# Longer rows and buffers for TensorE's float32r operands in a four-layer hybrid decoder trunk

## The chip, the core and the metric

The kernel runs on one core of a Trainium2 chip. The metric is the device time in microseconds (us) of one execution. TensorE (PE in the views) multiplies and transposes, and its weight loads are shown as an engine of their own (PEld). VectorE (DVE), ScalarE (ACT) and GpSimd (POOL) work elementwise, and SyncE's queue (SP) carries the weights from HBM.

## The reference, cut to what matters

A decoder of four layers works on 256 tokens of 1024 features in float32. Each layer adds a token mixer and an MLP to the running x:

```
for i in range(4):
    x = x + mixer[i % 3](rmsnorm(x) * norm1[i])     # retention, MoBA, differential, retention
    u = relu((rmsnorm(x) * norm2[i]) @ w_up[i])     # 1024 -> 4096
    x = x + (u * u) @ w_down[i]                     # 4096 -> 1024
```

Retention has four heads with keys of 256 and values of 512 features and a gate. The two attentions have sixteen heads of 64 features, a relative position bias and a norm of q and k per head. Each mixer has a projection in (1024 to 6144 or 3072) and one out.

## The kernel before, in words

**Precision.** The big products are made in float32r, TensorE's faster form of float32. To keep the accuracy, each operand is split into a high part (a copy rounded to float32r) and a low part (what is left). `passes` (L296) then issues three matmuls for each product: high by high, high weights by low moving, low weights by high moving. In every call of PE.matmul, lhsT is the stationary operand, which is loaded as weights (128 columns), and rhs is the moving operand that streams past it (256 or 512 columns).

**Weights.** `load_raw` brings one megabyte at a time into one of three buffers `raw`. `split_piece` (L153) lets ScalarE copy half of it into `whi`, `split_lo` (L167) lets VectorE subtract to get `wlo`. There are six buffers of each, 4096 bytes per partition, used in turn; `advance` keeps the split four pieces ahead of the matmuls.

**Activations.** The normed x is transposed and split into `xhi` and `xlo` (`norm_new` L262, `norm_quarter` L266), eight rows (k) of 256 tokens each, 1024 bytes per row. Retention and attention leave their output in `oh` and `ol` (four rows each). The MLP leaves the squared hidden units in `uu` (`act_u`, L375): rows 0 and 1 are high, 2 and 3 low.

**Which operand is which.** In `mm_a` (the up projection, `up`, and retention's q and k, `qk`), the weights are slices of `whi` and `wlo`, and a row of `xhi` or `xlo` moves, 256 columns. In `mm_b` (`vg` and `qkv`), slices of `xhi` and `xlo` are the weights, and `whi` or `wlo` moves, 512 columns. In `mm_o` (the projections out and down, `acc`), slices of `uu` or `oh` and `ol` are the weights, and `whi` or `wlo` moves, 512 columns. In retention's `av` (L444) the scores `s2` are the weights, and `vh` or `vl` moves, 512 columns; its output is called `o`.

**Order.** The order of all work is written out by hand (`manual_schedule`). The MLP does `up(s + 1)`, 48 matmuls, ahead of the 24 matmuls `acc` of slice s, so `uu` of one slice is made while the next slice's up projection runs. Small work (transposes `xt`, `oT`, `qkT`, attention scores `sc`, all in float32) is put between these runs by `later` and `tick`.

**Addresses.** The pools lie one behind the other in the order in which they are opened (const, op, xp, up, wp, mp, rp), and every tile takes a multiple of 32 bytes per partition. This puts the beginning of each of `oh`, `ol`, `xhi`, `xlo`, `uu`, `vh`, `vl`, `whi` and `wlo` at remainder 32 modulo 128, and the slices taken from them start at multiples of 512 bytes from there. Only `s2`, in the pool mp behind fifteen small tiles of 32 bytes, begins at remainder 0.

Of the kernel before, what the change touches and what calls it, by code (L numbers as in the profile page):

```python
# [10 lines left out]
F32R = mybir.dt.float32r  # L11
# [5 lines left out]
P = 128  # L17
S = 256
# [3 lines left out]
KC = D // P  # L22
# [9 lines left out]
def trunk(ctx, tc, x_in, rel_bias, norm1, norm2, w_up, w_down, ret_w_in, ret_w_out,  # L32
# [8 lines left out]
    op_ = ctx.enter_context(tc.tile_pool(name="op", bufs=1))  # L41
    xp = ctx.enter_context(tc.tile_pool(name="xp", bufs=1))
    up_ = ctx.enter_context(tc.tile_pool(name="up", bufs=1))
    wp = ctx.enter_context(tc.tile_pool(name="wp", bufs=1))
# [7 lines left out]
    NRAW, NPC = 3, 6  # L52
# [4 lines left out]
    def aux_bank(name):  # L57
        return pa.tile([P, 512], F32, tag="aux", name=name)
# [11 lines left out]
    def run_due():  # L70
        while True:
            due = [p for p in pending if p[0] <= clock[0]]
            if not due:
                return
            p = min(due, key=lambda p: p[:3])
            pending.remove(p)
            p[3](*p[4])

    def tick():
        clock[0] += 1  # L80
        run_due()


    specs = []

# [63 lines left out]
    def parts(i, n):  # L149
        m = n if i else n // 2  # L150
        return [slice(c, c + m) for c in range(0, n, m)]

    def split_piece():  # L153
        i = nxt[1]
        r = i // 2
        if r >= len(specs):
            return
        nxt[1] += 1
        _, a, b = specs[r]
        half = raws[r][:, (i % 2) * (a // 2):(i % 2 + 1) * (a // 2), :]  # L160
        hi = wp.tile([P, a // 2, b], F32R, tag="hi", name="whi", bufs=NPC)
        lo = wp.tile([P, a // 2, b], F32R, tag="lo", name="wlo", bufs=NPC)
        for part in parts(i, a // 2):
            ACT.activation(hi[:, part], half[:, part], AF.Copy)  # L164
        pieces[i] = (hi, lo, half)
# [13 lines left out]
    def advance(ah=4, al=4):  # L179
        while True:  # L180
            a, b = nxt[1], nxt[3]
            if nxt[1] <= nxt[2] + ah and nxt[1] // 2 < len(specs):
                split_piece()
            if nxt[3] <= nxt[2] + al:
                split_lo()
            if (a, b) == (nxt[1], nxt[3]):
                return
# [8 lines left out]
    rows = mp.tile([32, P], F32, tag="t2k", name="rows", bufs=4)  # L196
# [63 lines left out]
    st = {}  # L260

    def norm_new():  # L262
        st["hi"] = xp.tile([P, KC, S], F32R, tag="xhi", name="xhi")
        st["lo"] = xp.tile([P, KC, S], F32R, tag="xlo", name="xlo")

    def norm_quarter(l, which, c, t):  # L266
        tt = slice(t * P, (t + 1) * P)
# [33 lines left out]
    def mm_a(ps, half, first_of_phase=False):  # L301
        if not first_of_phase:
            advance()
        hi, lo = take()
        for m in range(2):
            for kk in range(4):
                k = half * 4 + kk
                passes(ps[:, m * S:(m + 1) * S], hi[:, kk, m * P:(m + 1) * P], lo[:, kk, m * P:(m + 1) * P],
                       st["hi"][:, k, :], st["lo"][:, k, :],
                       half == 0 and m == 0 and kk == 0, half == 1 and m == 1 and kk == 3)  # L310
                if first_of_phase and m == 0 and kk == 2:
                    tick()
        tick()
# [16 lines left out]
    def acc_new():  # L330
        st["acc"] = {q: mm_bank("acc") for q in QUARTERS}
# [9 lines left out]
    def out_piece(src, first):  # L341
        advance()
        pc = take()
        for q in QUARTERS:
            mm_o(q, pc, src, first, False)
        tick()

    def finish(srcs, r2, nxt_norm):
        advance(4, 4)
        pcs = [take() for _ in srcs]  # L350
        if nxt_norm is not None:
            norm_new()
        for q in QUARTERS:
            for i, (pc, src) in enumerate(zip(pcs, srcs)):
                mm_o(q, pc, src, False, i == len(srcs) - 1)
            c, t = q
            xs = X[:, t, c * 512:(c + 1) * 512]
            ps = st["acc"][q]
            if r2 is None:
                DVE.tensor_tensor(xs, ps, xs, op=OP.add)  # L360
            else:
                DVE.scalar_tensor_tensor(xs, ps, r2[:, t:t + 1], xs, op0=OP.mult, op1=OP.add)
            if nxt_norm is None:
                nc.sync.dma_start(out.rearrange("b s d -> (b s) d")[t * P:(t + 1) * P, c * 512:(c + 1) * 512], xs)
            else:
                later(2, norm_quarter, nxt_norm[0], nxt_norm[1], c, t)
            tick()
        if nxt_norm is not None:
            later(3, rms, nxt_norm[1])


    def mlp(l):
        U = {}

        def act_u(s, ps):  # L375
            u = mp.tile([P, 512], F32, tag="t2k", name="u", bufs=4)
            ACT.activation(u, ps, AF.Relu)  # L377
            DVE.scalar_tensor_tensor(u, ps, 0.0, u, op0=OP.max, op1=OP.mult)  # L378
            uu = up_.tile([P, 4, S], F32R, tag="p4k", name="uu", bufs=6)
            uh, ul = uu[:, 0:2, :], uu[:, 2:4, :]  # L380
            uf = u.rearrange("p (m s) -> p m s", m=2)
            ACT.activation(uh, uf, AF.Copy)
            DVE.tensor_tensor(ul, uf, uh.bitcast(F32), op=OP.subtract)
            U[s] = [(uh[:, m, :], ul[:, m, :]) for m in range(2)]

        def up(s):
            ps = aux_bank("up")
            mm_a(ps, 0, s == 0)
            mm_a(ps, 1)
            act_u(s, ps)  # L390

        up(0)
        acc = False
        for s in range(16):
            if s + 1 < 16:
                up(s + 1)
            if not acc:
                acc_new()
                acc = True
            if s < 14:  # L400
                for m in range(2):
                    out_piece(U[s][m], s == 0 and m == 0)
                del U[s]
            elif s == 14:
                out_piece(U[s][0], False)
            else:
                finish([U[14][1]] + U[15], st["r2"], (l + 1, 0) if l + 1 < DEPTH else None)


    def retention(l):  # L410
        OT = {}
        kd = mp.tile([P, 8, S], F32, tag="kd", name="kd")
# [61 lines left out]

        def to_feat(h, e, t):
            if h not in OT:
                OT[h] = (op_.tile([P, 4, S], F32R, tag="ot%d" % h, name="oh"),
                         op_.tile([P, 4, S], F32R, tag="ol%d" % h, name="ol"))
            ps = aux_bank("oT")
            for i in range(4):  # L480
                PE.transpose(ps[:, i * P:(i + 1) * P], e["go", t][:, i * P:(i + 1) * P], ident)
            v = ps.rearrange("p (i s) -> p i s", i=4)
            hi = OT[h][0][:, :, t * P:(t + 1) * P]
            lo = OT[h][1][:, :, t * P:(t + 1) * P]
            ACT.activation(hi, v, AF.Copy)
            DVE.tensor_tensor(lo, v, hi.bitcast(F32), op=OP.subtract)
# [31 lines left out]
        for c in range(13):  # L518
            h, i = divmod(c, 4)
            out_piece((OT[h][0][:, i, :], OT[h][1][:, i, :]), c == 0)  # L520
        finish([(OT[3][0][:, i, :], OT[3][1][:, i, :]) for i in (1, 2, 3)], None, (l, 1))
# [35 lines left out]
    def attention(l):  # L557
# [12 lines left out]
        def at(tk, fn, *a):  # L570
            later(max(t0 + 1 + tk - clock[0], 0), fn, *a)
        V = [up_.tile([P, D], F32, tag="p4k", name="vt", bufs=6) for _ in range(2)]
        OT = [(op_.tile([P, 4, S], F32R, tag="ot%d" % (2 + b), name="oh"),
               op_.tile([P, 4, S], F32R, tag="ol%d" % (2 + b), name="ol")) for b in range(2)]
        if diff:
            lambda_full()
        qs = qsc[:, 1:2] if diff else qsc[:, 0:1]
# [178 lines left out]


    norm_new()
    for t in range(2):
        norm_quarter(0, 0, 0, t)  # L760
    split_piece()
    split_lo()
    for t in range(2):
        later(1, norm_quarter, 0, 0, 1, t)
    later(1, split_piece)
    later(1, split_lo)
    later(3, rms, 0)
    later(10, head_weights)
    for l in range(DEPTH):
        if l % 3 == 0:  # L770
            retention(l)
        else:
            attention(l)
        mlp(l)
# [43 lines left out]
```

## Time and profile before

| | |
|---|---|
| median of 3 runs | 1371.81 us (1371.8 to 1372.04) |
| profiled execution, its own time | 1371.75 us |
| its span, first to last instruction | 1370.0 us |
| TensorE busy in the span | 1355.8 us, 99% |
| VectorE, ScalarE, GpSimd busy | 62%, 50%, 8% |
| mean granted TensorE clock | 0.999 of full speed |

The span is 1.75 us shorter than the execution's own time. A matmul's listed duration reaches from its start to a modelled end and overlaps the next one, so a run of matmuls is read by the distance between starts.

### The profile page before, as it was taken

The page shows a single profiled execution, that of the slowest core. Times are in us where ns is not written, and L with a number is a line of the kernel's source. Part 1 is how long each engine was busy: PE and PEld are TensorE (multiplying, and loading weights), DVE is VectorE, ACT ScalarE, POOL GpSimd, SP SyncE. Part 2 cuts the span into 40 slices and gives each one's busy share as a digit, 9 for nine tenths or more (in the row PEclk, how much of TensorE's full clock was granted, in tenths as well). Part 3 has the DMA queues.
Part 4 walks back from the last instruction along what each step waited for, and adds up shares of the span by engine and source line. Part 5 has one row for each costly group of instructions (what it writes and reads, how often), then busy time and mean ns, then how long its engine had stood idle before and what let it go on. Part 6 is the DMA issues. An engine that isn't in the chain of part 4 may idle for free.

```text
span 1370.0 us, 19714 instructions
## 1 busy us (share of the span) xinstructions
PE 1355.8 (99%) x7956; PEld 1190.5 (87%) x7956; DVE 846.8 (62%) x1246; ACT 689.6 (50%) x1063; POOL 109.1 (8%) x316
## 2 busy tenths in 40 slices
PE   7999999999999999999999999999999999999998
PEld 6888889999987779999987789999988888899997
DVE  6666647555568856555578675555667675555554
ACT  5454436444456645444466754444455444544442
POOL 3111100000032000000021100000031011000000
PEclk9999999999999999999999999999999999999999
DMA  8545464555565336555554346555564555465551
GB/s 279 178 159 180 163 206 159 188 189 190 195 208 167 124 123 219 185 185 184 185 173 136 123 154 215 185 185 184 169 207 144 180 182 188 151 216 186 185 185 62
DMA packets 140796, 242.26 MB, mean 177 GB/s; under 512 B 4256, under 2 KB 87920, under 8 KB 140704
## 3 DMA queue, kind: packets, MB, share of 16 engines
q1 hardware_dynamic: 137872, 236.99, 51.5%
q0 software_dynamic: 1072, 2.35, 0.6%
q10 hardware_dynamic: 1760, 1.66, 0.4%
q8 instruction: 62, 1.02, 0.3%
q14 instruction: 30, 0.25, 0.1%
HBM read 239.91 MB, written 1.07 MB: 176 GB/s over the span
## 4 chain that ended last, share of the span: by engine, by line
PE 98%; ACT 1%; DVE 0%; DMA 0%; issue 0%; ACTq 0%
PE acc L297 12%; PE acc L298 12%; PE acc L299 12%; PE up L299 9%; PE up L298 9%; PE up L297 9%; PE vg L297 4%; PE vg L299 4%; PE vg L298 4%; PE qkv L297 3%; PE qkv L299 3%; PE qkv L298 3%; PE qk L299 2%; PE qk L297 2%; PE qk L298 2%; PE sc L635 1%
## 5 line engine op out<-in xcount | busy, mean ns | idle before, releaser
L174 DVE TENSOR_TENSOR wlo<-raw,whi 128x1024 fp32r<-128x1024 f32 (+1 forms) x449 | 529.5, 1219 | 104.4 <-ACT whi L164 104.0
L164 ACT ACTIVATE whi<-raw 128x1024 fp32r<-128x1024 f32 (+1 forms) x449 | 451.8, 1051 | 89.4 <-PE acc L299 66.9
L297 PE MATMUL up<-xhi,whi 128*128 128x256 f32 x1024 | 290.1, 283 | 0.0
L299 PE MATMUL up<-xhi,wlo 128*128 128x256 f32 x1024 | 289.8, 283 | 0.0
L298 PE MATMUL up<-xlo,whi 128*128 128x256 f32 x1024 | 289.7, 283 | 0.0
L297 PE MATMUL acc<-whi,uu 128*128 128x512 f32 x512 | 200.5, 392 | 0.0
L298 PE MATMUL acc<-wlo,uu 128*128 128x512 f32 x512 | 199.9, 390 | 0.0
L299 PE MATMUL acc<-whi,uu 128*128 128x512 f32 x512 | 199.3, 389 | 0.0
L298 PEld LDWEIGHTS up<-xlo,whi 128*128 128x128 f32 x1024 | 196.3, 192 | 2.2
L297 PEld LDWEIGHTS up<-xhi,whi 128*128 128x128 f32 x1024 | 196.3, 192 | 2.2
L299 PEld LDWEIGHTS up<-xhi,wlo 128*128 128x128 f32 x1024 | 196.3, 192 | 0.0
L378 DVE SCALAR_TENSOR_TENSOR u<-up,u 128x512 f32<-128x512 f32 x64 | 44.2, 691 | 221.7 <-ACT u L377 221.6
L377 ACT ACTIVATE u<-up 128x512 f32<-128x512 f32 x64 | 38.1, 595 | 258.9 <-PE up L299 258.9
L299 PEld LDWEIGHTS acc<-whi,uu 128*128 128x128 f32 x512 | 96.1, 188 | 20.6
L297 PEld LDWEIGHTS acc<-whi,uu 128*128 128x128 f32 x512 | 96.4, 188 | 18.1
L298 PEld LDWEIGHTS acc<-wlo,uu 128*128 128x128 f32 x512 | 96.4, 188 | 17.6
L297 PE MATMUL vg<-whi,xhi 128*128 128x512 f32 x256 | 100.6, 393 | 0.0
L299 PE MATMUL vg<-whi,xlo 128*128 128x512 f32 x256 | 99.8, 390 | 0.0
L298 PE MATMUL vg<-wlo,xhi 128*128 128x512 f32 x256 | 99.7, 390 | 0.0
L297 PE MATMUL qkv<-whi,xhi 128*128 128x512 f32 x192 | 81.6, 425 | 0.0
L297 PE MATMUL acc<-whi,oh 128*128 128x512 f32 x192 | 76.4, 398 | 0.0
L297 PE MATMUL qk<-xhi,whi 128*128 128x256 f32 x256 | 73.8, 288 | 1.5 <-ACT whi L164 1.5
(215 smaller groups left out, 1823.5 us busy)
## 6 DMA issues: line engine op xcount, KB each, us to landing
raw<-in_w_up_dram SPq DMA_DIRECT2D x64, 1024.0 KB, 5.6
raw<-in_w_down_dram SPq DMA_DIRECT2D x64, 1024.0 KB, 6.1
raw<-in_ret_w_in_dram SPq DMA_DIRECT2D x47, 1024.0 KB, 5.3
raw<-in_ret_w_out_dram SPq DMA_DIRECT2D x16, 1024.0 KB, 5.0
raw<-in_moba_w_in_dram SPq DMA_DIRECT2D x12, 1024.0 KB, 5.2
raw<-in_diff_w_in_dram SPq DMA_DIRECT2D x12, 1024.0 KB, 5.3
raw<-in_moba_w_out_dram SPq DMA_DIRECT2D x4, 1024.0 KB, 4.8
raw<-in_diff_w_out_dram SPq DMA_DIRECT2D x4, 1024.0 KB, 5.0
```

What stands on the lines that cost most here:

```text
L164: ACT.activation(hi[:, part], half[:, part], AF.Copy)
L174: DVE.tensor_tensor(lo[:, part], half[:, part], hi[:, part].bitcast(F32), op=OP.subtract)
L297: PE.matmul(ps, lhsT=ah, rhs=bh, start=first, stop=False, skip_group_check=True)
L298: PE.matmul(ps, lhsT=ah, rhs=bl, start=False, stop=False, skip_group_check=True)
L299: PE.matmul(ps, lhsT=al, rhs=bh, start=False, stop=last, skip_group_check=True)
L377: ACT.activation(u, ps, AF.Relu)
L378: DVE.scalar_tensor_tensor(u, ps, 0.0, u, op0=OP.max, op1=OP.mult)
L635: PE.matmul(ps[:, :, :n], lhsT=QT[b][:, i, qt * P:(qt + 1) * P], rhs=KZ[b][:, i, :, :n], start=True, stop=True)
```

## The change

A helper, `staggered`, makes the float32r operand tiles longer. With rows=True each row of b elements is followed by 8 more (32 bytes), so the rows of `xhi`, `xlo`, `uu`, `oh` and `ol` are 1056 bytes apart and not 1024. Without it the whole buffer is 32 bytes longer, so the six buffers of `whi`, and those of `wlo`, are 4128 bytes apart and not 4096. The extra bytes are neither written nor read. `vh`, `vl` and `s2` stay as they were. All instructions keep their number and order.

```
+    def staggered(pool, shape, tag, name, bufs, rows=False):
+        a, b = shape
+        if rows:
+            return pool.tile([P, a, b + 8], F32R, tag=tag, name=name, bufs=bufs)[:, :, :b]
+        t = pool.tile([P, a * b + 8], F32R, tag=tag, name=name, bufs=bufs)
+        return t[:, :a * b].rearrange("p (a b) -> p a b", a=a)
...
-        hi = wp.tile([P, a // 2, b], F32R, tag="hi", name="whi", bufs=NPC)
-        lo = wp.tile([P, a // 2, b], F32R, tag="lo", name="wlo", bufs=NPC)
+        hi = staggered(wp, [a // 2, b], "hi", "whi", NPC)
+        lo = staggered(wp, [a // 2, b], "lo", "wlo", NPC)
...
-        st["hi"] = xp.tile([P, KC, S], F32R, tag="xhi", name="xhi")
-        st["lo"] = xp.tile([P, KC, S], F32R, tag="xlo", name="xlo")
+        st["hi"] = staggered(xp, [KC, S], "xhi", "xhi", 1, True)
+        st["lo"] = staggered(xp, [KC, S], "xlo", "xlo", 1, True)
...
-            uu = up_.tile([P, 4, S], F32R, tag="p4k", name="uu", bufs=6)
+            uu = staggered(up_, [4, S], "p4k", "uu", 6, True)
...
-                OT[h] = (op_.tile([P, 4, S], F32R, tag="ot%d" % h, name="oh"),
-                         op_.tile([P, 4, S], F32R, tag="ol%d" % h, name="ol"))
+                OT[h] = (staggered(op_, [4, S], "ot%d" % h, "oh", 1, True),
+                         staggered(op_, [4, S], "ol%d" % h, "ol", 1, True))
```

The tiles `oh` and `ol` of `attention` (L573) are changed in the same way.

## Rows read from the trace of the kernel before

**Rows 1.** The page: busy time of the engines, and TensorE's clock in 40 slices.

```profile
PE 1355.8 (99%) x7956; PEld 1190.5 (87%) x7956; DVE 846.8 (62%) x1246; ACT 689.6 (50%) x1063; POOL 109.1 (8%) x316
...
PEclk9999999999999999999999999999999999999999
```

**Rows 2.** Groups by line and form, PE: shapes, count, busy us, mean ns, idle before.

```profile
L297 PE MATMUL up<-xhi,whi 128*128 128x256 f32 x1024 | 290.1, 283 | 0.0
...
L297 PE MATMUL acc<-whi,uu 128*128 128x512 f32 x512 | 200.5, 392 | 0.0
...
L297 PE MATMUL vg<-whi,xhi 128*128 128x512 f32 x256 | 100.6, 393 | 0.0
...
L297 PE MATMUL qkv<-whi,xhi 128*128 128x512 f32 x192 | 81.6, 425 | 0.0
L297 PE MATMUL acc<-whi,oh 128*128 128x512 f32 x192 | 76.4, 398 | 0.0
...
L297 PE MATMUL qk<-xhi,whi 128*128 128x256 f32 x256 | 73.8, 288 | 1.5 <-ACT whi L164 1.5
...
L297 PE MATMUL o<-vh,s 128*128 128x512 f32 x24 | 9.6, 399 | 0.0
```

**Rows 3.** Timeline of PE, one slice of an MLP: start us, listed duration us.

```profile
605.47 0.28 PE L297 MATMUL up<-xhi,whi 128*128 128x256 f32 x1
...
605.82 0.28 PE L297 MATMUL up<-xhi,whi 128*128 128x256 f32 x1
...
611.10 0.28 PE L299 MATMUL up<-xhi,wlo 128*128 128x256 f32 x1
611.22 0.40 PE L297 MATMUL acc<-whi,uu 128*128 128x512 f32 x1
...
613.06 0.39 PE L299 MATMUL acc<-whi,uu 128*128 128x512 f32 x1
...
616.46 0.39 PE L299 MATMUL acc<-whi,uu 128*128 128x512 f32 x1
616.69 0.28 PE L297 MATMUL up<-xhi,whi 128*128 128x256 f32 x1
```

**Rows 4.** Timeline of PE, retention's second head, from vg to o and back.

```profile
73.23 0.39 PE L297 MATMUL vg<-whi,xhi 128*128 128x512 f32 x1
...
77.77 0.40 PE L299 MATMUL vg<-whi,xlo 128*128 128x512 f32 x1
78.00 0.39 PE L297 MATMUL o<-vh,s 128*128 128x512 f32 x1
...
80.10 0.39 PE L297 MATMUL vg<-whi,xhi 128*128 128x512 f32 x1
...
82.37 0.39 PE L298 MATMUL vg<-wlo,xhi 128*128 128x512 f32 x1
```

**Rows 5.** Timeline of PE, first layer of attention, qkv matmuls behind float32 scores.

```profile
432.23 0.40 PE L298 MATMUL qkv<-wlo,xhi 128*128 128x512 f32 x1
...
434.54 0.39 PE L299 MATMUL qkv<-whi,xlo 128*128 128x512 f32 x1
```

**Rows 6.** Timeline of PE, retention, qk matmuls behind float32 transposes.

```profile
57.38 0.28 PE L298 MATMUL qk<-xlo,whi 128*128 128x256 f32 x1
...
58.33 0.28 PE L297 MATMUL qk<-xhi,whi 128*128 128x256 f32 x1
...
59.41 0.28 PE L297 MATMUL qk<-xhi,whi 128*128 128x256 f32 x1
```

**Rows 7.** Groups by line and form, the instructions that write uu.

```profile
L383 DVE TENSOR_TENSOR uu<-u,uu 128x512 fp32r<-128x512 f32 x64 | 44.3, 692 | 44.7 <-ACT uu L382 44.7
L378 DVE SCALAR_TENSOR_TENSOR u<-up,u 128x512 f32<-128x512 f32 x64 | 44.2, 691 | 221.7 <-ACT u L377 221.6
L382 ACT ACTIVATE uu<-u 128x512 fp32r<-128x512 f32 x64 | 40.5, 632 | 51.9 <-DVE u L378 51.9
L377 ACT ACTIVATE u<-up 128x512 f32<-128x512 f32 x64 | 38.1, 595 | 258.9 <-PE up L299 258.9
```

More of the change, by code (lines that the diff above doesn't have):

```diff
@@ L572, in attention @@
         V = [up_.tile([P, D], F32, tag="p4k", name="vt", bufs=6) for _ in range(2)]
-        OT = [(op_.tile([P, 4, S], F32R, tag="ot%d" % (2 + b), name="oh"),
-               op_.tile([P, 4, S], F32R, tag="ol%d" % (2 + b), name="ol")) for b in range(2)]
+        OT = [(staggered(op_, [4, S], "ot%d" % (2 + b), "oh", 1, True),
+               staggered(op_, [4, S], "ol%d" % (2 + b), "ol", 1, True)) for b in range(2)]
         if diff:
```

## The prediction

> **What bounds the kernel now.** I read the page first. TensorE is busy 99% of the span, at the full clock (9 in every slice, the 2.4 GHz level), while VectorE and ScalarE have 62% and 50% [rows 1]. So the end is set by how fast TensorE gets through its matmuls, and anything that shortens or lengthens a matmul of the big products counts almost in full.
>
> The groups by line and form say how many there are [rows 2]. Each group of L297 has two sisters of the same count, L298 and L299, since `passes` issues three matmuls. With 256 columns that makes 3 x (1024 + 256) = 3840 (`up` and `qk`); with 512 columns 3 x (512 + 256 + 192 + 192) = 3456 (`acc` twice, `vg`, `qkv`), and 3 x 24 = 72 more for `o`. No group has idle time before it worth naming, so TensorE isn't waiting for anybody.
>
> What one of them costs is read from starts in the timeline. In one MLP slice, 44 `up` matmuls run from 605.82 to 611.10: 5.28 / 44 = 120.0 ns each. Fifteen `acc` matmuls run from 613.06 to 616.46: 3.40 / 15 = 226.7 ns [rows 3]. At 2.4 GHz and one column per tick, 256 columns are 106.7 ns and 512 are 213.3 ns, so both kinds pay the same 13.3 ns on top, whatever their length. Over 7296 matmuls that is 97 us, and it is all that this change can reach.
>
> **What the pace hangs on.** Three rows show that it isn't a constant.
>
> First, it settles. The first 8 `acc` matmuls of the slice take 611.22 to 613.06, 230.0 ns each, before the pace of 226.7 is reached [rows 3]. Behind float32 scores, ten `qkv` matmuls take 432.23 to 434.54, 231.0 ns each [rows 5]. Behind float32 transposes, eight `qk` matmuls take 57.38 to 58.33, 118.8 ns each, and the next nine, to 59.41, 120.0 ns [rows 6]. So the settled pace of 512 columns is better than the unsettled one, and that of 256 columns is slightly worse. Nothing but TensorE's own two streams (the moving operand of one matmul and the weight load of the next) repeats so exactly that it could settle.
>
> Second, the one place where the two streams have unequal remainders has another pace. In `o` the moving `vh` and `vl` begin at remainder 32 and the weights `s2` at 0; everywhere else in the big products both are at 32. The 20 `vg` gaps before it, 73.23 to 77.77, are 227.0 ns each; the nine matmuls of `o`, 78.00 to 80.10, take 233.3 ns each; the ten `vg` gaps from 80.10 to 82.37 are at 227.0 ns again [rows 4]. The listed durations say the same: 399 ns for the mean of `o` at L297 against 392 and 393 for `acc` and `vg` [rows 2].
>
> Third, 120.0, 226.7 and 233.3 ns are 18, 34 and 35 times 6.67 ns, which looks like two streams that fall into step.
>
> I take these together as: equal remainders let the two streams fall into step, and unequal ones gave 6.7 ns more in the only place where they occur. That `s2` is also in another pool is the weak point; nothing in the rows tells pool and remainder apart.
>
> **The change part by part.** *Instructions.* None is added, removed or moved, no DMA is touched, no wait is added. SBUF use grows by 12 x 32 for `whi` and `wlo`, 2 x 8 x 32 for `xhi` and `xlo`, 6 x 128 for the slots that `uu` shares, and 8 x 128 for `oh` and `ol`: 2688 bytes per partition, with every buffer count kept.
>
> *New remainders.* Row k of `xhi` and `xlo` begins at 32 + 32k, buffer b of `whi` at 32 + 32b, buffer b of `wlo` 64 further on (six buffers of 32 extra bytes lie between), row i of `uu`, `oh`, `ol` at 32 + 32i, all modulo 128. In one piece of `mm_a` the weights stay at one remainder while k goes through four: the distance between weights and moving operand takes 0, 32, 64 and 96 in turn, and L299's `wlo` adds 64. `mm_b` and `mm_o` mix likewise. So about one pair in four keeps equal remainders, and the pair changes from matmul to matmul. The 72 matmuls of `o` change neither.
>
> *512 columns.* One slice's 24 `acc` take 611.22 to 616.69 now, 227.9 ns on average with their settling [rows 3]. If they never settle, the nearest rows are 231.0 (equal, unsettled, [rows 5]) and 233.3 (unequal, [rows 4]). I take the middle, 232.2, since both kinds of pair occur: +4.3 ns x 3456 = +14.9 us. The ends: 231.0 gives +10.7, 233.3 gives +18.7.
>
> *256 columns.* 48 `up` take 605.47 to 611.22 now, 119.8 ns each [rows 3]. No row has unequal remainders here. If unsettled, the nearest row is 118.8 [rows 6]: -1.0 ns x 3840 = -4.0 us, the value I take, as it is the only row of this shape off its step. The ends: if they pay `o`'s 6.7 ns on the settled 120.0, 126.7, that is +6.9 x 3840 = +26.5 us; if they lose all of the 13.3 ns, -13.1 x 3840 = -50.3 us.
>
> *Writers of the tiles.* `uu` is now written as two rows of 256 with a gap and no longer as one run of 512, by ScalarE (632 ns) and VectorE (692 ns) [rows 7]. I cost this at nothing. Relu, square, copy and subtract take 595 + 691 + 632 + 692 = 2.6 us, and the 48 `up` matmuls of the next slice, 5.75 us [rows 3], stand between them and the `acc` that needs `uu`. Without that cover, a tenth more on both would be 0.13 us x 64 = 8.5 us. The writers of `xhi`, `oh` already write separate rows, and those of `whi` and `wlo` one run as before. If they were slower, `whi` would be late next, with ScalarE half idle.
>
> *Sum:* +14.9 - 4.0 = +10.9 us on the profiled execution's own 1371.75 us (span 1370.0 plus 1.75), which is 0.06 us from the median of the runs: **1382.7 us**, 0.8% slower.
>
> The Trainium skill has a rule for the pace ("TensorE: Matmul & The Clock Gate", Back-to-back issue gap): columns / 2.4 plus 2.5 ns, thus 215.8 and 109.2 ns. The trace shows 226.7 and 120.0 in its place [rows 3], 10.8 ns more in both; by that rule the reach of any address change would be an estimated 79 us and not the 97 above.
>
> **The rivals.** *No change.* The two streams don't see each other's addresses, and `o` is slow for another reason, such as its pool or its having only nine matmuls to settle in. For it: settling behind float32 work gives 231.0 with equal remainders too [rows 5]. Against it: `o` starts straight out of a settled `vg`, and `vg` behind it is settled at once [rows 4], so a step was not lost but shifted. Time: 1371.8 us. Here the Trainium skill speaks ("SBUF — State Buffer", Who interferes with whom): TensorE has two independent read ports, one for the moving operand and one for weight loads, and never waits on anyone. By that rule the remainders are of no account and this rival is the outcome; the three paces above don't agree with it.
>
> *Faster: the collisions get fewer.* The 13.3 ns would be the two streams meeting in the same part of the memory because they start alike; spread starts would avoid part of the meetings. It is decided in `up`, at a pace below 118.8 ns there with `acc` no slower than 227.9. For it: the unsettled `qk` are already faster than the settled ones [rows 6]. Against it: the only unequal pair is slower [rows 4]. Half of the 13.3 ns gone is 6.7 x 7296 = -49 us, 1323 us; all of it, 1275 us; 256 columns alone at 117 ns, -2.8 x 3840 = -11 us, 1361 us.
>
> *Slower twice over: 256 columns pay `o`'s price as well.* +18.7 + 26.5 = +45 us, 1417 us. For it: both shapes pay the same 13.3 ns now. Against it: off their step, 256 columns are faster, not slower [rows 6].
>
> **How the numbers follow.** Chances: forecast 0.43, no change 0.17, faster 0.27, twice over 0.13. The forecast's own range is 1376 to 1391 us: the lower end has 512 columns at 231.0 and 256 at 118.8 with a few settled, the upper has 233.3 and 256 columns as now. For 8 in 10 the range takes in no change, the part of the faster case down to two thirds of its half-way price (-32 us), and most of the way to twice over: 1340 to 1408 us. A change under 0.2% (2.7 us) can't be told from none; by that bound faster has 0.27, the same 0.17, slower 0.43 + 0.13 = 0.56.
>
> **What the profile after would show.** Right: TensorE still at 99% and full clock; `acc` starts in an MLP slice about 232 ns apart without ever settling at 226.7, `up` at 118 to 119 ns and no longer an even 120.0; `o` at 233.3 as before; listed means of `acc` and `vg` near 396 to 399 ns; writers of `uu` within a tenth of 632 and 692 ns. No change would show 120.0 and 226.7 again. The forecast is wrong if some distance between the remainders is better than 0, which no row here has, or if a mixed order finds a step of its own: then `acc` or `up` shows paces below 226.7 or 118.

## The result and the profile after

The changed kernel takes 1379.34 us (median of 4 runs, 1379.11 to 1380.03) against 1371.92 us for the kernel before on the same chip: 1.0054 times as long, 95% interval 1.0042 to 1.0066, or 7.4 us more. The forecast was 1382.7 us.

The page after: busy time of each engine. The span is 1377.3 us.

```profile
PE 1362.9 (99%) x7956; PEld 1184.3 (86%) x7956; DVE 847.3 (62%) x1246; ACT 690.1 (50%) x1063; POOL 108.9 (8%) x316
...
PEclk9999999999999999999999999999999999999999
```

Everything beside TensorE is as it was [rows 1]: the same number of instructions, the same clock, VectorE and ScalarE within 0.5 us. The groups by line and form after, the lines that answer to [rows 2] and [rows 7] (all line numbers are 8 higher):

```profile
L305 PE MATMUL up<-xhi,whi 128*128 128x256 f32 x1024 | 287.8, 281 | 0.0
...
L305 PE MATMUL acc<-whi,uu 128*128 128x512 f32 x512 | 203.0, 397 | 0.0
...
L305 PE MATMUL vg<-whi,xhi 128*128 128x512 f32 x256 | 101.7, 397 | 0.0
...
L305 PE MATMUL acc<-whi,oh 128*128 128x512 f32 x192 | 77.2, 402 | 0.0
...
L305 PE MATMUL qk<-xhi,whi 128*128 128x256 f32 x256 | 73.3, 286 | 1.5 <-ACT whi L172 1.5
...
L305 PE MATMUL o<-vh,s 128*128 128x512 f32 x24 | 9.6, 399 | 0.0
...
L391 DVE TENSOR_TENSOR uu<-u,uu 128x512 fp32r<-128x512 f32 x64 | 44.3, 693 | 44.7 <-ACT uu L390 44.7
L390 ACT ACTIVATE uu<-u 128x512 fp32r<-128x512 f32 x64 | 40.5, 633 | 51.9 <-DVE u L386 51.9
```

In these listed durations, matmuls of 256 columns became 2 ns shorter, those of 512 columns 4 to 5 ns longer; `o` stayed at 399 ns and the writers of `uu` at 692 to 693 and 632 to 633 ns. The timeline of PE for the same MLP's slice after, to be read beside [rows 3] by the distance between starts:

```profile
609.21 0.28 PE L305 MATMUL up<-xhi,whi 128*128 128x256 f32 x1
...
614.85 0.39 PE L305 MATMUL acc<-whi,uu 128*128 128x512 f32 x1
...
616.93 0.40 PE L305 MATMUL acc<-whi,uu 128*128 128x512 f32 x1
...
620.40 0.28 PE L305 MATMUL up<-xhi,whi 128*128 128x256 f32 x1
```

The 48 `up` take 5.64 us (117.5 ns each, 119.8 before), the 24 `acc` 5.55 us (231.3 ns, 227.9 before). The last fifteen `acc` take 3.47 us, 231.3 ns each: the settled 226.7 ns is gone.

For the whole trace I took the distance from each float32r matmul's start to the next float32r matmul's (breaks over 260 and 150 ns left out, the 72 matmuls of `o` counted with the 512 columns). This mean is called the pace below. It went from 227.97 to 232.03 ns for 512 columns and from 119.83 to 118.13 ns for 256. Summed by use, each start to the next matmul of any kind, in us:

| | before | after | change |
|---|---|---|---|
| `up` | 368.8 | 363.6 | -5.2 |
| `qk` | 95.2 | 94.0 | -1.2 |
| `acc` from `uu` | 350.3 | 357.0 | +6.7 |
| `acc` from `oh` | 133.1 | 135.5 | +2.4 |
| `vg` | 175.6 | 178.6 | +3.0 |
| `qkv` | 139.3 | 141.1 | +1.8 |

Added up before rounding, the sum is +7.4 us. The MLPs are nearly even (-5.2 and +6.7); the mixers, where 512 columns prevail, carry the loss.

### The profile page after: what moved, and what is told of

It is laid out like the page before. It is cut to its first block, busy times and chain, and to the rows that moved or that the text cites. A ratio compares the mean times of both kernels' runs of the same rounds, so it can differ in the third digit from the quotient of the medians.

```text
span 1377.3 us, 19714 instructions
## 1 busy us (share of the span) xinstructions
PE 1362.9 (99%) x7956; PEld 1184.3 (86%) x7956; DVE 847.3 (62%) x1246; ACT 690.1 (50%) x1063; POOL 108.9 (8%) x316
## 4 chain that ended last, share of the span: by engine, by line
PE 98%; ACT 1%; DVE 0%; DMA 0%; issue 0%; ACTq 0%
PE acc L305 12%; PE acc L306 12%; PE acc L307 12%; PE up L305 9%; PE up L307 9%; PE up L306 9%; PE vg L305 4%; PE vg L306 4%; PE vg L307 4%; PE qkv L305 3%; PE qkv L307 3%; PE qkv L306 3%; PE qk L307 2%; PE qk L305 2%; PE qk L306 2%; PE sc L643 1%
## 5 line engine op out<-in xcount | busy, mean ns | idle before, releaser
L305 PE MATMUL acc<-whi,uu 128*128 128x512 f32 x512 | 203.0, 397 | 0.0
L307 PE MATMUL acc<-whi,uu 128*128 128x512 f32 x512 | 200.9, 392 | 0.0
L305 PEld LDWEIGHTS up<-xhi,whi 128*128 128x128 f32 x1024 | 192.7, 188 | 2.5
L306 PEld LDWEIGHTS up<-xlo,whi 128*128 128x128 f32 x1024 | 192.6, 188 | 2.5
L307 PEld LDWEIGHTS up<-xhi,wlo 128*128 128x128 f32 x1024 | 192.6, 188 | 0.0
L306 PE MATMUL acc<-wlo,oh 128*128 128x512 f32 x192 | 75.8, 395 | 0.0
```

Of the source, the lines that this page charges most:

```text
L305: PE.matmul(ps, lhsT=ah, rhs=bh, start=first, stop=False, skip_group_check=True)
L306: PE.matmul(ps, lhsT=ah, rhs=bl, start=False, stop=False, skip_group_check=True)
L307: PE.matmul(ps, lhsT=al, rhs=bh, start=False, stop=last, skip_group_check=True)
```

## The experiments

I call **distance** the address of the weights that are loaded during a matmul, less the address of that matmul's moving operand. The weights loaded during a matmul are taken to be those of the next one, and the addresses are those in the built program. The theory that follows from the prediction is that the distance sets the pace (*theory of the distance*). Its rival is that a constant distance, whatever it is, lets the streams fall into step, and only its changing from matmul to matmul costs (*theory of the mixture*). A third is that addresses aren't the cause at all.

### Constant distances: 32, 64 and 96 bytes

A tile of 32 bytes times n ahead of `whi` moves all `whi` and `wlo`, and a second one makes up 128 bytes with it, so that the pools behind keep their remainders modulo 128 (two small memsets on GpSimd are added):

```
+    wpad = wp.tile([P, 8 * n], F32, tag="wpad", name="wpad")         # n = 1, 2, 3
+    mpad = mp.tile([P, 32 - 8 * n], F32, tag="mpad", name="mpad")
+    POOL.memset(wpad, 0.0)
+    POOL.memset(mpad, 0.0)
```

> The kernel before with the pool of whi and wlo moved up by 32 bytes, so that these begin at remainder 64 and everything that meets them at 32, always the same distance. Theory of the mixture (the change costs because the distance alters from matmul to matmul, so the two streams never fall into step): a constant distance settles again, acc at 226.7 ns and up at 120.0 ns, time within 0.2% of 1371.9 us. Theory of the distance (unequal remainders themselves cost what o pays): acc, vg, qkv at 233.3 ns throughout, +5.4 ns x 3456 = +18.7 us, 1390 us, with up unknown between 118 and 127 ns. No effect of addresses: 226.7 and 120.0.

> As the run with 32 bytes, with whi and wlo at remainder 96, 64 from their partners. Theory of the mixture: settled paces of 226.7 and 120.0 ns, 1371.9 us. Theory of the distance: a pace of its own that stays constant over a whole acc stretch, between 224 and 236 ns; at 233.3 ns 1390 us.

> As the run with 32 bytes, with whi and wlo at remainder 0, so that in acc the weights lie 32 above the moving operand and in up 32 below it. Theory of the mixture: 226.7 and 120.0 ns, 1371.9 us. Theory of the distance: up now has the order that o has (weights 32 below the moving operand) and goes from 120.0 to about 126.7 ns, +26 us, while acc takes the other sign, unknown between 224 and 236 ns.

| | `up`, `qk`: distance, pace | `acc`, `vg`, `qkv`: distance, pace | median us | ratio to before |
|---|---|---|---|---|
| before | 0, 119.8 | 0, 228.0 | 1372.3 | |
| 32 apart | +32, 118.4 | -32, 233.2 | 1384.5 | 1.0089 [1.0074, 1.0104] |
| 64 apart | +64, 116.0 | -64, 229.6 | 1358.4 | 0.9905 [0.9884, 0.9925] |
| 96 apart | +96, 118.6 | -96, 233.3 | 1385.8 | 1.0100 [1.0083, 1.0116] |

The timeline of PE, 32 apart: one `acc` stretch and the `up` stretch behind it.

```profile
606.22 0.39 PE L301 MATMUL acc<-whi,uu 128*128 128x512 f32 x1
...
611.81 0.28 PE L301 MATMUL up<-xhi,whi 128*128 128x256 f32 x1
...
617.50 0.39 PE L301 MATMUL acc<-whi,uu 128*128 128x512 f32 x1
```

The distance doesn't change here, and still the 24 `acc` take 5.59 us, 232.9 ns each. The theory of the mixture asked for 226.7. So it falls in this form, and the theory of the distance holds, with `o`'s price for -32 everywhere (233.2 forecast as 233.3). The total stayed under its 1390 us because `up` and `qk`, which it left open, got 1.4 ns faster. Its guess for 96, that `up` would pay as `o` does, was wrong: 256 columns got faster at all three distances.

At 64, four runs lay between 1356.45 and 1363.5 us. The timeline of the profiled one (1363.5) shows that `up` has two paces at one distance; the other three have no trace.

```profile
604.62 0.28 PE L301 MATMUL up<-xhi,whi 128*128 128x256 f32 x1
...
610.27 0.40 PE L301 MATMUL acc<-whi,uu 128*128 128x512 f32 x1
...
923.19 0.28 PE L301 MATMUL up<-xhi,whi 128*128 128x256 f32 x1
...
928.66 0.39 PE L301 MATMUL acc<-whi,uu 128*128 128x512 f32 x1
```

The 48 `up` take 5.65 us (117.7 ns) in the second layer and 5.47 us (114.0 ns) in the third. In this run all `up` stretches to the second layer's end had the slower pace; in the third and fourth layers only the first stretch had it (117.6 and 117.7 ns), and all others 113.8 or 113.9. `acc` changed with it, from 229.7 to 228.9 ns. Had the first two layers run like the last two, the run would have been an estimated 6 us shorter (3.9 ns for each of some 1500 `up`). That is most of the spread of the four runs, but for the others it isn't shown.

### The same remainders modulo 128, other addresses

```
+        t = pool.tile([P, a * b + 32], F32R, tag=tag, name=name, bufs=bufs)
+        return t[:, :a * b].rearrange("p (a b) -> p a b", a=a)
...
+        hi = staggered(wp, [a // 2, b], "hi", "whi", NPC)
+        lo = staggered(wp, [a // 2, b], "lo", "wlo", NPC)
```

> The buffers of whi and wlo are 128 bytes longer in place of 32, rows as before: they move apart, but all remainders modulo 128 stay at 32. Both theories of remainders: 226.7 and 120.0 ns, within 0.2% of 1371.9 us. If it is the spacing of the buffers, or any address bit above 128, that costs: up to the +7.4 us of the change.

1378.19 us, 1.0043 [1.0028, 1.0058]: slower, though the remainders modulo 128 stayed as they were, so both theories are wrong in the form with 128. Sorted by distance, the pace for 512 columns is 228.8 ns at 0, 228.6 at 256, 232.2 at 128 and 232.9 at 384. For 512 columns 256 bytes are as good as none, and 128 are not: **the pattern repeats every 256 bytes**, not every 128. For 256 columns 0 and 256 agree too (both 119.6), but 128 has 119.3 and 384 has 118.3, so for them the period rests on 0 and 256 alone. Distances are given modulo 256 from here on.

### Is it the address that makes o slow?

```
+    mpad = mp.tile([P, 8], F32, tag="mpad", name="mpad")
+    POOL.memset(mpad, 0.0)
```

> The kernel before with the pool mp moved up by 32 bytes inside, so that s2, the weights of o, begin at remainder 32 as their moving vh and vl do. If the distance of the addresses makes o slow, its matmuls come down from 233.3 ns to the settled 226.7 ns when they follow vg directly; if its pool or its shortness does, they stay at 233.3. Total time the same to 0.5 us either way.

The timeline of PE in this kernel, the stretch that answers to [rows 4]:

```profile
78.53 0.39 PE L299 MATMUL o<-vh,s 128*128 128x512 f32 x1
...
80.57 0.39 PE L299 MATMUL vg<-whi,xhi 128*128 128x512 f32 x1
```

Nine matmuls in 2.04 us, 226.7 ns each, where the kernel before needs 2.10. Over all 72 matmuls of `o` the mean went from 233.2 to 227.4 ns. Beside the added memset only addresses moved: `s2` and everything else in the pools mp and rp lie 32 bytes higher; the pool of `s2`, the length of `o` and its neighbours stayed. The median is 1371.81 us (one run).

### A ruler of 16 bytes, and one of 4

Each buffer of `whi` and `wlo` is 256 bytes longer, and a piece starts an offset into it that depends on its slice s:

```
+            offs[len(specs)] = 4 * s          # elements; in up(s) and down(s) of spec_mlp
...
+        n, o = a // 2 * b, offs.get(r, 0)
+        hi = wp.tile([P, n + 64], F32R, tag="hi", name="whi", bufs=NPC)
+        lo = wp.tile([P, n + 64], F32R, tag="lo", name="wlo", bufs=NPC)
+        hi, lo = [x[:, o:o + n].rearrange("p (a b) -> p a b", b=b) for x in (hi, lo)]
```

The finer ruler has 9 + s for `up` and 0 for `acc` in layers 0 and 1, and 0 for `up` and s for `acc` in layers 2 and 3.

> A ruler: buffers of whi and wlo 256 bytes longer, and in slice s of each MLP both hi and lo start 16 s bytes into the buffer, for up as for acc, so that each stretch of 48 and of 24 matmuls has one constant distance, 0 to 240 bytes in steps of 16. Theory of the distance modulo 256, from the runs so far: up at 120.0 ns for 0, 118.3 for 32, 116.0 for 64, 118.6 for 96; acc (weights that far below the moving operand) at 227.9 with settling for 0, 233.2 for 32, 229.6 for 64, 233.3 for 96, about 232 for 128; the other distances are not known. Theory of the mixture: every stretch settles at 120.0 and 226.7. No total is forecast.

> A finer ruler, buffers 256 bytes longer. Layers 0 and 1: up's pieces start 36 + 4 s bytes in (36 to 96), acc's at 0. Layers 2 and 3: up's at 0, acc's 4 s bytes in (weights 0 to 60 below the moving operand). Theory of the distance: up between 117.4 and 118.5 ns away from 64 and at 113.3 or 117.8 near it, the two paces that were seen at 64; acc between 226.7 and 235. If the memory works in units of 32 bytes, distances within one unit have one pace; in units of 16, four neighbours have one; if each is different, the step is 4 bytes.

The timeline of PE under the first ruler: up at 64, acc at -48; up at 128; acc at -208.

```profile
549.73 0.28 PE L301 MATMUL up<-xhi,whi 128*128 128x256 f32 x1
...
555.17 0.39 PE L301 MATMUL acc<-whi,uu 128*128 128x512 f32 x1
...
560.70 0.28 PE L301 MATMUL up<-xhi,whi 128*128 128x256 f32 x1
...
594.43 0.28 PE L301 MATMUL up<-xhi,whi 128*128 128x256 f32 x1
...
600.20 0.39 PE L301 MATMUL acc<-whi,uu 128*128 128x512 f32 x1
...
667.60 0.40 PE L301 MATMUL acc<-whi,uu 128*128 128x512 f32 x1
...
673.23 0.28 PE L301 MATMUL up<-xhi,whi 128*128 128x256 f32 x1
```

That is 113.3 ns for `up` and 230.4 for `acc`; 120.2 for `up`; 234.6 for `acc`. Each of the four layers gives the same pace for the same slice within 0.1 ns (slice 0 and the last slices apart, which are mixed with their neighbours).

The timeline of PE under the finer ruler: up at 52, and up at 56.

```profile
547.74 0.28 PE L301 MATMUL up<-xhi,whi 128*128 128x256 f32 x1
...
553.51 0.39 PE L301 MATMUL acc<-whi,uu 128*128 128x512 f32 x1
...
558.98 0.28 PE L301 MATMUL up<-xhi,whi 128*128 128x256 f32 x1
...
564.63 0.40 PE L301 MATMUL acc<-whi,uu 128*128 128x512 f32 x1
```

That is 120.2 and 117.7 ns for addresses 4 bytes apart. The means of both rulers in ns (the values at 0 are those of the kernel before):

```
distance mod 256:    0    16    32    48    64    80    96   112   128   144   160   176   192   208   224   240
256 columns      119.8 118.4 118.3 117.8 113.5 118.6 117.5 119.6 120.0 118.3 119.7 118.0 117.8 116.8 116.7 117.3
512 columns      227.9 231.4 232.7 234.6 233.4 231.0 233.7 233.2 232.4 231.0 233.3 231.6 229.3 230.0 233.3 231.4

distance mod 256:   44    48    52    56    60    64    68    72    76    80    84    88    92    96
256 columns      117.7 118.4 120.0 117.8 119.6 117.8 118.4 118.4 113.6 118.6 120.0 113.8 118.3 117.3
```

For 512 columns, equal addresses are the best of all distances in steps of 16; of those 4 bytes apart, down to -52, one is level with them (-28 with 227.7) and the worst is -4 with 237.7. For 256 columns equal addresses are nearly the worst. Neighbours 4 bytes apart differ, so plateaus of 16 or 32 bytes don't exist here. The bounds of the finer ruler's forecast were missed on both sides: `up` has 113.6 to 120.0 away from 64, not 117.4 to 118.5, and `acc` goes above 235. Both rulers' totals (1372.53 and 1372.39 us, one run each) add up good and bad distances and mean nothing by themselves.

### Halves of the change

Only the rows (`xhi`, `xlo`, `uu`, `oh`, `ol`), and only the buffers (`whi`, `wlo`), with the change's own lines. The ruler's paces can now be added up, pair by pair, for any kernel.

> Half of the change: only the rows of xhi, xlo, uu, oh and ol are 32 bytes longer, whi and wlo as before. If a pair's pace is that of its own distance modulo 256, as the ruler measured it for constant distances, adding these paces up over all pairs of this kernel gives 231.9 ns for 512 columns and 117.9 for 256, +6.4 us, 1378.3 us. If changing the distance from matmul to matmul costs by itself, it is slower than that by more than 3 us (1381 us and up). If the longer buffers alone made the change slow, 1371.9 us.

> The other half: only the buffers of whi and wlo are 32 bytes longer. The same sum of the ruler's paces gives 231.6 ns and 117.8 ns, +4.9 us, 1376.8 us. Here the distance stays the same through half a piece's hi or lo and alters between hi and lo, so a cost of the mixing itself would be smaller than with rows only. If the longer rows alone made the change slow, 1371.9 us.

Rows only: 1377.1 us, 1.0039 [1.0025, 1.0053], paces 231.9 and 117.6 ns (forecast 231.9 and 117.9). Buffers only: 1380.77 us, 1.0066 [1.0051, 1.0081], paces 232.1 and 118.4 (forecast 231.6 and 117.8). Either half does it, and the two don't add up, as a distance that is spread over all values by one of them can't be spread further by the other. For the whole change the same sum gives 231.6 and 118.1 ns, +5.7 us, against 232.0 and 118.1 and +7.4 us measured.

So in total a mixture costs about the mean of its distances. Pair by pair it doesn't. In the changed kernel the pairs of 512 columns at distance 0 take 231.1 ns (227.9 when the distance is constant) and those at 64 take 231.5 (233.4); pairs of 256 columns take 117.5 at 0 (119.8) and 117.5 at 64 (113.5). Mixing draws all distances together, to 231.1 to 233.2 and 117.3 to 118.9 ns: good ones lose and bad ones gain. So the changing from matmul to matmul, which the theory of the mixture named, does count, and the sum of the ruler's paces is borne out for the mean alone.

The rows, where the distance changes most often, came out 1 us under the sum. The buffers came out 4 us over it, which stays unexplained. A possible reason is that a distance can have more than one pace (64 above; 96 gave 117.5 under the ruler and 118.6 in the run with 96).

### A better version

The distance for `up` and `qk` can be chosen apart from the others, since their pieces of `whi` and `wlo` are their own: offset d for these, 0 for all others, buffers 256 bytes longer. d is 16, 19 or 22 elements:

```
+            offs[len(specs)] = 19                               # in up(s)
+                offs[len(specs)] = offs[len(specs) + 1] = 19    # retention's two qk pieces per head
```

> Buffers of whi and wlo 256 bytes longer; pieces that are weights of 256-column matmuls (up and qk) start 64 bytes into them, all others at 0. Theory of the distance modulo 256: up and qk at 116.0 ns as with everything 64 apart, -3.8 x 3840 = -14.6 us, and acc, vg, qkv settled at 226.7 ns as before, together 1357 us. If the spacing of the buffers by itself costs (4352 bytes in place of 4096), acc goes to 231 ns and takes back up to +12 us. Theory of the mixture: 1371.9 us, as all distances are constant in a stretch.

> As the version with 64, but up and qk at 76 bytes, one of the two distances at which the finer ruler saw up settle at 113.3 ns behind acc at 0. If the pace belongs to the distance: 113.6 with settling, -6.2 x 3840 = -23.8 us, 1348 us, faster than every kernel so far. If it has two settled paces as 64 has and the start decides, up or qk stay near 118 in part: 1349 to 1364 us. If only the shape of the ruler gave it: 1364 us.

> The same with 88 bytes, the other distance that settled at 113.3 ns: 113.8 with settling, -6.0 x 3840 = -23.0 us, 1349 us; with two paces by the start 1350 to 1364 us; with neither 1364 us.

| offset | pace, 256 columns | pace, 512 columns | median us | ratio to before |
|---|---|---|---|---|
| 64 bytes | 117.7 | 227.9 | 1363.89 | 0.9940 [0.9924, 0.9957] |
| 76 bytes | 113.6 | 227.9 | 1348.47 | 0.9829 [0.9813, 0.9846] |
| 88 bytes | 114.4 | 227.9 | 1351.54 | 0.9851 [0.9836, 0.9865] |

The timeline of PE with 76 bytes, one slice, to be read beside [rows 3]:

```profile
607.13 0.28 PE L302 MATMUL up<-xhi,whi 128*128 128x256 f32 x1
...
612.59 0.40 PE L302 MATMUL acc<-whi,uu 128*128 128x512 f32 x1
...
614.65 0.39 PE L302 MATMUL acc<-whi,uu 128*128 128x512 f32 x1
...
618.05 0.28 PE L302 MATMUL up<-xhi,whi 128*128 128x256 f32 x1
```

5.46 us for 48 `up`, 113.8 ns each, and 5.46 us for 24 `acc`, 227.5 ns: both shapes at their good pace. 64 bytes missed its forecast of 1357 us, because behind `acc` at 0 all `up` stretches took the slower of 64's two paces. 76 bytes met its forecast of 1348 us and beats the kernel before by 1.7% and the changed one by more. 88 bytes came out 2.5 us over its 1349: most `up` stretches have 113.8 ns, but the first of three layers has 116.8 to 119.8, and `qk` has 115.2 in most heads. The longer buffers cost nothing: the last fifteen `acc` take 3.40 us, 226.7 ns each, with buffers 4352 bytes apart, 17 times 256.

## Why the prediction was right

**The bound.** Right: TensorE was still busy 99%, and the sum over its starts, +7.4 us, is the whole of the result.

**512 columns.** Forecast 227.9 to 232.2 ns, +14.9 us. Measured 227.97 to 232.03, +14.0 us over 3456 matmuls. The settled 226.7 was lost, as forecast.

**256 columns.** Forecast -1.0 ns, -4.0 us, from the one row off its step. Measured -1.7 ns, -6.5 us over 3840 matmuls. This term was mis-sized and makes most of the difference between 10.9 and 7.4 us. The pace of equal addresses before they settle [rows 6], 118.8 ns, stood in for distances that no row had; the mean over the eight multiples of 32 in the ruler is 117.9 ns, nearer to what the changed kernel has. For 512 columns the same mean is 232.0. In the slice shown `up` has 117.5 ns, under the 118 that the prediction named as a sign of being wrong; over the whole kernel it has 118.1, just inside.

**Equal and unequal remainders.** That `o` is slow for its 32 bytes was the weak point, and moving `s2` shows that it holds. The listed durations that the prediction called in beside it (399 ns against 392 and 393) don't tell: in the same [rows 2] `acc` from `oh` has 398 and `qkv` 425 with equal remainders. The prediction took remainders modulo 128, and about one pair in four as equal. Counted in the changed program, 25% of the pairs of 256 columns and 41% of those of 512 are equal modulo 128; modulo 256, where the pattern repeats, they are 13% and 22%. Equal pairs of 512 columns no longer settle, as forecast: they take 231.1 ns, against the 231.0 of the row it used. But unequal isn't one thing at 233.3 ns; constant distances in steps of 16 bytes have 229.3 to 234.6, and the unequal pairs of the changed kernel average 232.3. That the middle of two rows, 232.2, came within 0.2 ns of the measured mean is luck in part.

**Falling into step.** Some settled paces fit the 6.67 ns of the prediction: 113.3 is 17 steps, and 228.9 (settled `acc` at -64) is three matmuls in 103 steps, with gaps of 226, 229 and 232 ns in turn. Others, such as 118.4 ns at 32, fit no simple number, so a common step isn't shown, nor what would have it. The formula of the Trainium skill that the prediction set beside its sum ("TensorE: Matmul & The Clock Gate", Back-to-back issue gap) is given there for a matmul standing alone; in these streams of weight load and matmul no distance came down to its 109.2 or 215.8 ns.

**Writers.** Right: 693 and 633 ns, hidden as before.

**The rivals.** *No change* falls with the run that moves `s2`: 32 bytes, 233.3 to 226.7 ns. The rule of the Trainium skill that was its reason ("SBUF — State Buffer", Who interferes with whom), two independent read ports and no waiting, doesn't account for this run: addresses moved, those of the weights `s2` among them, and the matmuls that run beside their loads changed pace. What slows them is not shown. *Twice over* falls: no distance tried makes 256 columns pay `o`'s price; the slowest has 120.0 ns. *Faster* was half right about the mechanism: spread addresses do make the 256 columns faster (-6.5 us). It loses because equal addresses were nearly the worst case for one of the two shapes and, level with -28, the best for the other. The line in the prediction that some distance might be better than 0 came true for 256 columns alone, and the large gain, to 113.6 ns, only where one distance is kept.

**Left open.** The distance alone doesn't set the pace. The two rulers show it for `acc` at -48, where `whi`, `wlo` and `uu` lie at the same remainders modulo 256: the first ruler has 230.4 ns (555.17 to 560.70, above), the finer one 233.3.

```profile
953.38 0.39 PE L301 MATMUL acc<-whi,uu 128*128 128x512 f32 x1
...
958.98 0.28 PE L301 MATMUL up<-xhi,whi 128*128 128x256 f32 x1
```

What differs, beside slice and buffers, is the distance of the `up` stretch ahead, 64 and 0. At 64 `up` likewise has 113.5 ns under the first ruler and 117.8 under the finer one, again at the same remainders. So the matmuls that went before seem to matter; which of them pick the pace was not tried. Nor was a distance for the high and low parts apart, or one distance at other addresses of both operands.

## What to carry to other kernels

Where TensorE is busy all the time and its matmuls still stand further apart than their columns explain, read the distance between starts for each shape: a constant excess (here 13.3 ns for 256 and 512 columns alike) can depend on where the next matmul's weights and this one's moving operand lie. Don't spread addresses over all values; that only buys the mean of good and bad. Measure the pace by distance with a ruler such as the one above, give every shape its own constant distance, and measure that kernel again, since a distance can have another pace behind other matmuls: here 76 bytes for 256 columns and 0 for 512 took 1.7% off a kernel whose engine was 99% busy.

## What the runs showed that I had not expected

The pace of float32r matmuls depends on the address distance between two operands, and 4 bytes make a difference: the means go from 113.5 to 120.0 ns for 256 columns, and from 227.7 to 237.7 ns (at -4 bytes) for 512. One and the same distance can have two steady paces (64: 117.8 and 113.9 ns for 256 columns), and a run can change from one to the other between two layers. Runs of the kernel with 64 bytes differ by 7 us without any change in the program.
